# A two-layer hybrid diffusion trunk: branch A's GpSimd instructions placed on VectorE and ScalarE

## The chip, the cores and the metric

The kernel runs on one core of a Trainium2 chip. Its time is the device time of one execution in microseconds (us). Five engines work side by side, each through its own queue in order: TensorE (PE, with its weight loads shown as PEld), VectorE (DVE), ScalarE (ACT), GpSimd (POOL) and SyncE (SP, which issues most DMAs). An engine waits on semaphores for what another engine or a DMA must deliver. Before the change the median of three runs is 2233.82 us (2230.44 to 2238.89).

## The reference

One inference step of two trunk layers over 384 tokens (128 of context, 256 latent) with 2048 features in fp32. Each layer modulates its input, multiplies it by one wide input projection, feeds three branches, gates them, joins them, multiplies by an output projection and normalises. Cut to what matters here:

```python
u = x * (1.0 + scale[:, None]) + shift[:, None]
proj = jnp.matmul(u, lp['w_in'])            # 2048 x 8976
y_a = rwkv_mixer(...)    # A: 8 heads x 64, two directions
y_b = mlstm_mixer(...)   # B: 4 heads x 128, two directions
y_c = diff_attn_mixer(...)  # C: 8 heads, two softmaxes each
out = jnp.matmul(jnp.concatenate([y_a, y_b, y_c], axis=-1), lp['w_out'])
x_new = layer_norm(DEEPNORM_ALPHA * x + gate[:, None] * out, ...)

# branch A, one direction, one token (rwkv_scan):
sk = jnp.einsum('bhvk,bhk->bhv', S, kk_t)
S = S * w_t[:, :, None, :] - sk[..., None] * (kk_t * a_t)[:, :, None, :] + v_t[..., None] * k_t[:, :, None, :]
y_t = jnp.einsum('bhvk,bhk->bhv', S, r_t)
# and, beside the scan, the product of the same position:
bonus = bonus + jnp.sum(r * kt * lp['rwkv_r_k'], axis=-1, keepdims=True) * v
```

## The kernel before, in words

The two projections carry nearly all of the arithmetic. Their fp32 weights arrive in pieces of 512 KB (tile `raw`). ScalarE rounds half a piece to fp32r (`hi<-raw`) and VectorE, or for every fourth half piece GpSimd, takes the remainder (`lo<-raw,hi`). TensorE then makes three products for each block, hi times hi, hi times lo and lo times hi, into an accumulator `acc`; they are called the large products here. Everything else that TensorE does writes to a rotating PSUM tile `mx`, apart from the modulation (`ada`).

Branch A turns the token by token scan into chunks of 64 tokens. A unit is one chunk in one direction; there are 6 chunks and 2 directions, so 12 units in each layer and 24 in all. A unit passes through four streams, each of which may run ahead of the next:

- `a_front` (stream AF, line 1048) makes the decays (`th`, `q`), their products with the keys and values (tiles named `GE` and `QH` in the rows) and the product of the same position (`Tt`, `ci`, `big`), multiplies them on TensorE and masks the result into `Xo` and `Xd`. After its twelfth unit it scales four blocks and multiplies them with `VC`, which gives the bonus.
- `a_blocks` (AD, line 1166) inverts 8x8 blocks on VectorE by a chain of small instructions (`own`, `Xc`, `xr`, `tm`, `Di`).
- `a_inverse` (AI, line 1195) extends that to 64x64 by small matmuls, ScalarE copies and VectorE sums (tile `mixed`).
- `a_scan` (A, line 1236) carries the state `S` and adds up the output.

Before the change GpSimd makes the products for the upper 64 partitions of `GE` and `QH`, the product of the same position, the two differences `Xo - Xd` and `Xd - own`, and the copies into `LP` (the inputs of a unit) and `UV` (its values).

The order in which the instructions stand in the queues is found while the program is built. Every instruction passes through line 155, so all rows carry that line and are told apart by tile names. A planner (`spend`, line 265) keeps one clock for each engine with a price for each kind of instruction (`cost`, line 237). After each piece of the large products, `pump` (line 372) places a segment of a waiting stream (C's attention, A's four streams, evacuations) if its engine is free by these clocks, and places none while VectorE's or ScalarE's clock is more than `SLACK` ahead of TensorE's (line 377). At a few places the order is forced: `drain` (line 407) runs the ready streams, oldest first and with no large product between them, until the named stream has ended. One such place is `b_first` (line 1443), which calls `drain("AF")` because branch B's queries take the memory of `KR` that `a_front` reads. It stands in each layer behind the last key projection of C. The prices for VectorE, ScalarE and GpSimd differ, so moving an instruction to another engine changes the order of everything that the planner places.

Of the kernel before, what the change touches and what calls it, by code (L numbers as in the profile page):

```python
# [15 lines left out]
OP = mybir.AluOpType  # L16
# [34 lines left out]
PESHARE = 2000.0, 2000.0  # L51
HEAD = ("PG", 2), ("QHt", 2), ("Tt", 2), ("BK", 1), ("QH", 1), ("UV", 1), ("ce00", 1), ("ce10", 1)
MIX = "cccqqqvvvvq", "cccqqqvvvvq"
# [73 lines left out]
def bc(ap, shape):  # L127
    return ap.to_broadcast(list(shape))
# [73 lines left out]
class Hybrid:  # L202
# [845 lines left out]
    def a_front(self):  # L1048

        nc = self.nc  # L1050
        rev = slice(None, None, -1)
        lo, hi = slice(0, 64), slice(64, 128)
        fl = lambda x: x.rearrange("p a b -> p (a b)")

        def inputs(u):
            d, c = self.A_ORDER[u]
            for j, r in enumerate((lo, hi)):
                nc.gpsimd.tensor_copy(self.LP[r, j, :], self.LW[r, d, 64 * c:64 * c + 64])

        inputs(0)  # L1060

        wait = [self.mt([128, 4, 64], "Tt", bufs=2) for _ in range(2)]
        wait += [self.KR[:, :, 0, 64 * i:64 * i + 64] for i in range(2)]
        first = {}
        yield
        for u, (d, c) in enumerate(self.A_ORDER):
            ts = slice(64 * c, 64 * c + 64)
# [19 lines left out]
            BK = self.mt([128, 4, 2, 64], "BK")  # L1087
# [10 lines left out]
            Ea = E[:, :, d:64 + d], E[:, :, 1 - d:65 - d]  # L1098
            EQ = self.mt([128, 4, 64], "q1")
# [3 lines left out]

            PG = self.mt([128, 4, 4, 64], "GE", bufs=2)
            pgv = PG[lo, 0:3:2], PG[hi, 1:3]
            for e, r in enumerate((lo, hi)):
                (nc.gpsimd if e else nc.vector).tensor_tensor(PG[r, e], Ea[0][r], self.KR[r, :, 0, ts], OP.mult)
            nc.vector.tensor_tensor(PG[:, 2], Ea[1], self.KR[:, :, 1, ts], OP.mult)
            WL = self.mt([128, 4], "WL", bufs=2)
            self.act(WL, civ[:, :, last], AF.Exp, scale=-DECAY)  # L1110
            QH = self.mt([128, 4, 2, 64], "QH")
            for e, r in enumerate((lo, hi)):
                eqb = bc(EQ[r].unsqueeze(2), [64, 4, 2, 64])
                if e == 0:
                    nc.vector.tensor_tensor(QH[r], eqb, BK[r], OP.mult)
                else:
                    nc.gpsimd.tensor_tensor(QH[r][:, :, rev, :], eqb, BK[r], OP.mult)
            if c not in first:
                pd = first[c] = wait[{0: 0, 1: 1, 2: 0, 5: 1, 3: 2, 4: 3}[c]]
                nc.gpsimd.tensor_tensor(pd, BK[:, :, 1, :], self.KR[:, :, 1, ts], OP.mult)  # L1120
            else:
                pd = self.mt([128, 4, 64], "ci")
                nc.gpsimd.tensor_tensor(pd, BK[:, :, 1, :], self.KR[:, :, 1, ts], OP.mult)
                nc.gpsimd.tensor_tensor(self.KR[:, :, 1, ts], pd, first[c], OP.add)
            if u < 11:
                inputs(u + 1)
            yield
            pg = [self.mxp() for _ in range(2)]
            for p in range(4):
                for e, r in enumerate((lo, hi)):  # L1130
                    nc.tensor.matmul(pg[e][:, 128 * p:128 * p + 128], QH[r, p].rearrange("k a b -> k (a b)"),
                                     pgv[e][:, :, p, :], start=True, stop=True)
            GE = self.mt([128, 2, 4, 64], "PG", bufs=2)
            Xd = self.mt([128, 4, 64], "Xd", bufs=2)
            Xo = self.mt([128, 4, 64], "Xo", bufs=2)
# [8 lines left out]
            pq = [self.mxp() for _ in range(2)]  # L1144
            for e, r in enumerate((lo, hi)):
                for p in range(4):
                    nc.tensor.transpose(pq[e][:, 64 * p:64 * p + 64], QH[r, p].rearrange("k a b -> k (a b)"), self.ident[r, r])
            for e in range(2):
                nc.scalar.copy(QHt[:, e], pq[e][:, 0:256].rearrange("p (a b) -> p a b", a=4))
            bm = bc(self.k("bm16").unsqueeze(1), [128, 4, 64])  # L1150
            nc.vector.tensor_tensor(Xd, Xo, bm, OP.mult)
            nc.gpsimd.tensor_tensor(Xo, Xo, Xd, OP.subtract)
            self.fronts[u] = (Xd, Xo)
            self.units[u] = (PG, GE, QHt, WL)
            self.nf = u + 1
# [10 lines left out]
    def a_blocks(self):  # L1166


        nc = self.nc
        b8 = self.k("bm8")  # L1170
        for u, (d, c) in enumerate(self.A_ORDER):
            Xd, Xo = self.fronts.pop(u)
            own = self.mt([128, 4, 64], "own")
            nc.vector.tensor_tensor(own, Xd, bc(b8.unsqueeze(1), [128, 4, 64]), OP.mult)
            Xc = self.mt([128, 4, 8], "Xc")
            nc.vector.tensor_reduce(Xc, own.rearrange("p a (q t) -> p a t q", q=8), AX.X, OP.add)
            Di = self.mt([128, 4, 8], "Di", bufs=2)
            nc.vector.tensor_copy(Di, bc(self.k("i8").unsqueeze(1), [128, 4, 8]))
            nc.gpsimd.tensor_tensor(Xd, Xd, own, OP.subtract)
            yield  # L1180
            for n, s in enumerate(range(7) if d == 0 else range(7, 0, -1)):
                xr = self.mt([128, 4, 8], "xr")
                nc.vector.stream_shuffle(xr, Xc, [8 * i + s for i in range(4) for _ in range(8)])
                t2 = slice(s + 1, 8) if d == 0 else slice(0, s)
                w = 7 - s if d == 0 else s
                tm = self.mt([128, 4, 8], "tm")
                nc.vector.tensor_tensor(tm[:, :, 0:w], bc(Di[:, :, s:s + 1], [128, 4, w]), xr[:, :, t2], OP.mult)
                nc.vector.tensor_tensor(Di[:, :, t2], Di[:, :, t2], tm[:, :, 0:w], OP.add)
                if n % 3 == 2 and n < 6:
                    yield  # L1190
            self.blocks[u] = (Xd, Xo, Di)
            self.nd = u + 1
            yield
# [42 lines left out]
    def a_scan(self):  # L1236

        nc = self.nc
        lo, hi = slice(0, 64), slice(64, 128)
        ysum = self.mixed[:, 4:8, :]  # L1240
        v4 = lambda x: x.rearrange("p (a b) -> p a b", a=4)
        for u, (d, c) in enumerate(self.A_ORDER):
            ts = slice(64 * c, 64 * c + 64)
            UV = self.mt([128, 2, 4, 64], "UV")
            S = self.S[d, 0 if c < 2 else 1]
            for e, (ur, vr) in enumerate(((lo, hi), (hi, lo))):
                nc.scalar.copy(UV[ur, e], S[ur])
                nc.gpsimd.tensor_copy(UV[vr, e], self.VT[vr, c])
            yield
            PG, GE, QHt, WL, Tt = self.units.pop(u)  # L1250
            pr = self.mxp()
# [253 lines left out]
    def b_main(self):  # L1505
# [17 lines left out]
        nc.vector.tensor_scalar(nf, f, -1.0, None, OP.mult)  # L1523
        gr = [self.mt([4, T], ("QHt", "QH")[d], bufs=(2, 1)[d]) for d in range(2)]
        br = [self.mt([4, T], ("UV", "th")[d]) for d in range(2)]
# [567 lines left out]
```

## Time and profile before

| | |
|---|---|
| median of three runs | 2233.82 us |
| profiled execution, time | 2234.41 us |
| its span, first to last instruction | 2232.7 us |
| PE / PEld busy | 2131.0 us (95%) / 1875.6 us (84%) |
| DVE / ACT / POOL busy | 1376.1 us (62%) / 950.1 us (43%) / 651.1 us (29%) |
| mean granted TensorE clock | 0.983 of full speed |

Busy times are sums of instruction durations, so a busy PE is not PE at its peak. Branch A's units lie in two stretches, from about 190 to 760 us (layer 0) and from about 1290 to 1810 us (layer 1). In a grouped row the two numbers behind the bar are the sum in us and the mean in ns, and then the engine's idle time just before and what ended it.

### The profile page before, as it was taken

The page shows a single profiled execution, that of the slowest core. Times are in us where ns is not written, and L with a number is a line of the kernel's source. Part 1 is how long each engine was busy: PE and PEld are TensorE (multiplying, and loading weights), DVE is VectorE, ACT ScalarE, POOL GpSimd, SP SyncE. Part 2 cuts the span into 40 slices and gives each one's busy share as a digit, 9 for nine tenths or more (in the row PEclk, how much of TensorE's full clock was granted, in tenths as well). Part 3 has the DMA queues.
Part 4 walks back from the last instruction along what each step waited for, and adds up shares of the span by engine and source line. Part 5 has one row for each costly group of instructions (what it writes and reads, how often), then busy time and mean ns, then how long its engine had stood idle before and what let it go on. Part 6 is the DMA issues. An engine that isn't in the chain of part 4 may idle for free. (4 is left out here: it accounts for less than half of the span.)

```text
span 2232.7 us, 44851 instructions
## 1 busy us (share of the span) xinstructions
PE 2131.0 (95%) x17261; PEld 1875.6 (84%) x17261; DVE 1376.1 (62%) x3704; ACT 950.1 (43%) x2215; POOL 651.1 (29%) x930
## 2 busy tenths in 40 slices
PE   6999999999999999999998999999999999999998
PEld 3778878778778788889997998787888789999997
DVE  2667766766675523578338677776776754367634
ACT  3345344353343533445326453444444354344543
POOL 3111433324332211111435223242343312111344
PEclk9999999999999999999998999999999999999998
DMA  9995433433434464554465442223232224333444
GB/s 323 317 320 148 135 112 110 128 100 108 148 99 137 151 194 155 171 154 152 153 198 185 137 123 91 78 76 105 70 93 79 78 83 152 114 114 118 141 146 144
DMA packets 313791, 314.83 MB, mean 141 GB/s; under 512 B 17569, under 2 KB 309030, under 8 KB 313450
## 3 DMA queue, kind: packets, MB, share of 16 engines
q1 hardware_dynamic: 305450, 299.49, 43.1%
q0 software_dynamic: 3616, 10.22, 1.4%
q8 instruction: 136, 2.23, 0.4%
q10 hardware_dynamic: 4512, 2.26, 0.4%
q14 instruction: 77, 0.63, 0.1%
HBM read 298.81 MB, written 13.12 MB: 140 GB/s over the span
## 5 line engine op out<-in xcount | busy, mean ns | idle before, releaser
L155 PE MATMUL acc<-uh,hi 128*128 128x384 f32 x2240 | 808.0, 361 | 11.6 <-ACT uh L155 7.7
L155 PE MATMUL acc<-uh,lo 128*128 128x384 f32 x2240 | 763.0, 341 | 5.8 <-POOL lo L155 3.4
L155 PE MATMUL acc<-ul,hi 128*128 128x384 f32 x2240 | 762.9, 341 | 1.3 <-DVE ul L155 1.3
L155 DVE TENSOR_TENSOR lo<-raw,hi 128x512 fp32r<-128x512 f32 (+1 forms) x496 | 361.8, 739 | 519.2 <-ACT hi L155 508.7
L155 ACT CAST hi<-raw 128x512 fp32r<-128x512 f32 (+1 forms) x659 | 395.7, 618 | 401.3 <-PE acc L155 259.4
L155 POOL TENSOR_TENSOR lo<-raw,hi 128x512 fp32r<-128x512 f32 (+1 forms) x163 | 221.9, 1361 | 927.3 <-ACT hi L155 860.0
L155 PEld LDWEIGHTS acc<-uh,hi 128*128 128x128 f32 x2240 | 426.6, 190 | 76.4 <-issue 35.8
L155 PEld LDWEIGHTS acc<-uh,lo 128*128 128x128 f32 x2240 | 425.3, 190 | 9.2 <-DVE lo L155 4.9
L155 PEld LDWEIGHTS acc<-ul,hi 128*128 128x128 f32 x2240 | 426.2, 190 | 6.0 <-DVE ul L155 3.1
L155 PE MATMUL acc<-hi,uh 128*128 128x256 f32 (+1 forms) x768 | 226.5, 295 | 2.8 <-ACT hi L155 1.1
L155 PE MATMUL acc<-lo,uh 128*128 128x256 f32 (+1 forms) x768 | 216.8, 282 | 1.0 <-DVE lo L155 1.0
L155 PE MATMUL acc<-hi,ul 128*128 128x256 f32 (+1 forms) x768 | 216.1, 281 | 0.0
L155 PEld LDWEIGHTS acc<-hi,uh 128*128 128x128 f32 x768 | 144.5, 188 | 20.3 <-issue 10.9
L155 PEld LDWEIGHTS acc<-lo,uh 128*128 128x128 f32 x768 | 144.6, 188 | 1.8 <-DVE lo L155 1.8
L155 PEld LDWEIGHTS acc<-hi,ul 128*128 128x128 f32 x768 | 144.7, 188 | 0.0
L155 ACT ACTIVATE ce<-mx,cmx 128x384 f32<-128x384 f32 (+1 forms) x96 | 48.0, 505 | 113.2 <-DVE cmx L155 110.1
L155 PE MATMUL ada<-raw,sil 128*32 128x256 f32 x1088 | 88.4, 399 | 1.8 <-DMA raw<-in_w_ada_dram 1.8
L155 ACT COPY mixed<-mx 64x256 f32<-64x256 f32 x120 | 44.0, 366 | 104.4 <-PE mx L155 102.7
L155 PEld LDWEIGHTS mx<-mixed 128*64 128x64 f32 x1536 | 53.5, 139 | 26.3 <-issue 11.1
L155 PE MATMUL mx<-mixed 128*64 128x64 f32 x1536 | 66.9, 230 | 3.3 <-DVE mixed L155 2.9
L155 DVE TENSOR_TENSOR mixed<-mx,mixed 128x256 f32<-128x256 f32 (+1 forms) x96 | 40.1, 418 | 30.1 <-PE mx L155 29.7
L155 DVE TENSOR_REDUCE cmx<-mx 128x1 f32<-128x384 f32 (+1 forms) x96 | 40.4, 460 | 19.8 <-PE mx L155 19.5
(435 smaller groups left out, 2940.5 us busy)
## 6 DMA issues: line engine op xcount, KB each, us to landing
raw<-in_w_in_dram SPq DMA_DIRECT2D x224, 512.0 KB
raw<-in_w_ada_dram SPq DMA_DIRECT2D x136, 512.0 KB
raw<-in_w_out_dram SPq DMA_DIRECT2D x64, 512.0 KB
big<-in_w_ada_dram SPq DMA_DIRECT2D x42, 512.0 KB
raw<-in_w_in_dram SPq DMA_DIRECT2D x32, 520.0 KB
GE<-in_w_ada_dram SPq DMA_DIRECT2D x14, 512.0 KB
cq<-xs SPq DMA_DIRECT2D x32, 192.0 KB
big<-in_w_in_dram SPq DMA_DIRECT2D x21, 256.0 KB
```

Of the source, the lines that this page charges most:

```text
L155: r = f(*args, **kw)
```

## The change

Branch A has no instruction on GpSimd any more apart from clearing. VectorE now makes `GE` and `QH` for all 128 partitions at once, the product of the same position and both differences. ScalarE copies the upper half of `GE` and of `QH` into the order that the matmul of the upper half reads (`QH` has three parts for it), and makes the copies into `LP` and `UV`. The shapes that TensorE reads stay as they are.

```diff
--- before.py
+++ after.py
@@ -1055,7 +1055,7 @@
         def inputs(u):
             d, c = self.A_ORDER[u]
             for j, r in enumerate((lo, hi)):
-                nc.gpsimd.tensor_copy(self.LP[r, j, :], self.LW[r, d, 64 * c:64 * c + 64])
+                nc.scalar.copy(self.LP[r, j, :], self.LW[r, d, 64 * c:64 * c + 64])
 
         inputs(0)
 
@@ -1103,32 +1103,30 @@
 
             PG = self.mt([128, 4, 4, 64], "GE", bufs=2)
             pgv = PG[lo, 0:3:2], PG[hi, 1:3]
-            for e, r in enumerate((lo, hi)):
-                (nc.gpsimd if e else nc.vector).tensor_tensor(PG[r, e], Ea[0][r], self.KR[r, :, 0, ts], OP.mult)
+            nc.vector.tensor_tensor(PG[:, 0], Ea[0], self.KR[:, :, 0, ts], OP.mult)
+            nc.scalar.copy(PG[hi, 1], PG[hi, 0])
             nc.vector.tensor_tensor(PG[:, 2], Ea[1], self.KR[:, :, 1, ts], OP.mult)
             WL = self.mt([128, 4], "WL", bufs=2)
             self.act(WL, civ[:, :, last], AF.Exp, scale=-DECAY)
-            QH = self.mt([128, 4, 2, 64], "QH")
-            for e, r in enumerate((lo, hi)):
-                eqb = bc(EQ[r].unsqueeze(2), [64, 4, 2, 64])
-                if e == 0:
-                    nc.vector.tensor_tensor(QH[r], eqb, BK[r], OP.mult)
-                else:
-                    nc.gpsimd.tensor_tensor(QH[r][:, :, rev, :], eqb, BK[r], OP.mult)
+
+            QH = self.mt([128, 4, 3, 64], "QH")
+            nc.vector.tensor_tensor(QH[:, :, 0:2, :], bc(EQ.unsqueeze(2), [128, 4, 2, 64]), BK, OP.mult)
+            nc.scalar.copy(QH[hi, :, 2, :], QH[hi, :, 0, :])
+            qh = lambda e, p: QH[(lo, hi)[e], p, e:e + 2, :].rearrange("k a b -> k (a b)")
             if c not in first:
                 pd = first[c] = wait[{0: 0, 1: 1, 2: 0, 5: 1, 3: 2, 4: 3}[c]]
-                nc.gpsimd.tensor_tensor(pd, BK[:, :, 1, :], self.KR[:, :, 1, ts], OP.mult)
+                nc.vector.tensor_tensor(pd, BK[:, :, 1, :], self.KR[:, :, 1, ts], OP.mult)
             else:
                 pd = self.mt([128, 4, 64], "ci")
-                nc.gpsimd.tensor_tensor(pd, BK[:, :, 1, :], self.KR[:, :, 1, ts], OP.mult)
-                nc.gpsimd.tensor_tensor(self.KR[:, :, 1, ts], pd, first[c], OP.add)
+                nc.vector.tensor_tensor(pd, BK[:, :, 1, :], self.KR[:, :, 1, ts], OP.mult)
+                nc.vector.tensor_tensor(self.KR[:, :, 1, ts], pd, first[c], OP.add)
             if u < 11:
                 inputs(u + 1)
             yield
             pg = [self.mxp() for _ in range(2)]
             for p in range(4):
                 for e, r in enumerate((lo, hi)):
-                    nc.tensor.matmul(pg[e][:, 128 * p:128 * p + 128], QH[r, p].rearrange("k a b -> k (a b)"),
+                    nc.tensor.matmul(pg[e][:, 128 * p:128 * p + 128], qh(e, p),
                                      pgv[e][:, :, p, :], start=True, stop=True)
             GE = self.mt([128, 2, 4, 64], "PG", bufs=2)
             Xd = self.mt([128, 4, 64], "Xd", bufs=2)
@@ -1144,12 +1142,12 @@
             pq = [self.mxp() for _ in range(2)]
             for e, r in enumerate((lo, hi)):
                 for p in range(4):
-                    nc.tensor.transpose(pq[e][:, 64 * p:64 * p + 64], QH[r, p].rearrange("k a b -> k (a b)"), self.ident[r, r])
+                    nc.tensor.transpose(pq[e][:, 64 * p:64 * p + 64], qh(e, p), self.ident[r, r])
             for e in range(2):
                 nc.scalar.copy(QHt[:, e], pq[e][:, 0:256].rearrange("p (a b) -> p a b", a=4))
             bm = bc(self.k("bm16").unsqueeze(1), [128, 4, 64])
             nc.vector.tensor_tensor(Xd, Xo, bm, OP.mult)
-            nc.gpsimd.tensor_tensor(Xo, Xo, Xd, OP.subtract)
+            nc.vector.tensor_tensor(Xo, Xo, Xd, OP.subtract)
             self.fronts[u] = (Xd, Xo)
             self.units[u] = (PG, GE, QHt, WL)
             self.nf = u + 1
@@ -1176,7 +1174,7 @@
             nc.vector.tensor_reduce(Xc, own.rearrange("p a (q t) -> p a t q", q=8), AX.X, OP.add)
             Di = self.mt([128, 4, 8], "Di", bufs=2)
             nc.vector.tensor_copy(Di, bc(self.k("i8").unsqueeze(1), [128, 4, 8]))
-            nc.gpsimd.tensor_tensor(Xd, Xd, own, OP.subtract)
+            nc.vector.tensor_tensor(Xd, Xd, own, OP.subtract)
             yield
             for n, s in enumerate(range(7) if d == 0 else range(7, 0, -1)):
                 xr = self.mt([128, 4, 8], "xr")
@@ -1245,7 +1243,7 @@
             S = self.S[d, 0 if c < 2 else 1]
             for e, (ur, vr) in enumerate(((lo, hi), (hi, lo))):
                 nc.scalar.copy(UV[ur, e], S[ur])
-                nc.gpsimd.tensor_copy(UV[vr, e], self.VT[vr, c])
+                nc.scalar.copy(UV[vr, e], self.VT[vr, c])
             yield
             PG, GE, QHt, WL, Tt = self.units.pop(u)
             pr = self.mxp()
```

VectorE's queue at the first unit of layer 0, difference of the two programs (`q` holds the inverse decays, `big` the normalised keys and the receptance, `BK` the scaled keys):

```order
 L155 SCALAR_TENSOR_TENSOR BK_2390<-BK_2390,big_343_1767 128x4x64
 L155 SCALAR_TENSOR_TENSOR BK_2390<-th_2308,big_342_1766 128x4x64
-L155 TENSOR_TENSOR GE_2426<-th_2394,big_342_1766 64x256
-L155 TENSOR_TENSOR GE_2426<-th_2394,big_342_1766 128x256
-L155 TENSOR_TENSOR QH_2432<-q_448_2397,BK_2390 64x512
+L155 TENSOR_TENSOR GE_2426<-th_2394,big_342_1766 128x256 x2
+L155 TENSOR_TENSOR QH_2432<-q_448_2397,BK_2390 128x4x128
+L155 TENSOR_TENSOR Tt_2301<-BK_2390,big_342_1766 128x256
 L155 TENSOR_TENSOR lo_2448<-raw_2377,hi_2447 128x512
 L155 TENSOR_TENSOR lo_2452<-raw_2377,hi_2451 128x512
```

Two 64-partition products became parts of 128-partition ones, and the product of the same position (`Tt`) stands on VectorE ahead of the next remainders (`lo`).

ScalarE's queue at the same unit, after the change:

```order
L155 ACTIVATE q_448_2397<-ci_2352 128x256
L155 COPY GE_2426<-GE_2426 64x256
L155 ACTIVATE WL_2430<-ci_2352 128x4
L155 COPY QH_2432<-QH_2432 64x4x64
L155 COPY LP_1770<-mixed_1765 64x64 x2
L155 CAST hi_2447<-raw_2377 128x512
```

The four copies (one each into `GE` and `QH`, two into `LP`) are new on this queue and stand ahead of the next rounding (`hi`).

TensorE's queue at the forced place in layer 1, behind the last key projection of C, before the change (`mx` are small matmuls, here a step of A's inverse; `ada` the modulation; `acc` the large products):

```order
L155 MATMUL acc_20655<-ul_126,hi_20878 128x384
L155 MATMUL acc_20655<-uh_125,lo_20879 128x384
L155 MATMUL mx_21014<-mixed_14454 64x64 x8
L155 MATMUL ada_19307<-raw_20652,sil 32x256 x4
L155 MATMUL acc_21053<-uh_125,hi_20908 128x384
L155 MATMUL acc_21053<-ul_126,hi_20908 128x384
L155 MATMUL acc_21053<-uh_125,lo_20909 128x384
```

Eight small matmuls and four of the modulation stand between two large products.

The same place after the change, twelve rows from the middle of what stands between the same two large products (`ce`, `ck`, `cq` and `cvv` belong to C's attention, `mixed`, `UV`, `GE` and `big` to A):

```order
L155 MATMUL mx_20889<-mixed_14454 64x64 x8
L155 MATMUL mx_20899<-const,ce_4073_20842 128x128
L155 MATMUL mx_20906<-mixed_14454 64x64 x8
L155 MATMUL mx_20916<-big_2793_14455,const 128x384
L155 MATMUL mx_20919<-cvv_19914,ce_4074_20844 128x128
L155 MATMUL mx_20923<-const,ce_4086_20880 128x128
L155 MATMUL mx_20926<-mixed_14454 64x64 x8
L155 MATMUL mx_20951<-ck_20742,cq_20366 128x384
L155 MATMUL mx_20952<-ck_20742,cq_20366 128x384
L155 MATMUL mx_20962<-cvv_19914,ce_4087_20882 128x128
L155 MATMUL mx_20966<-UV_20936,GE_20260 64x64 x8
L155 MATMUL mx_20976<-big_2793_14455,const 128x384
```

`a_front` has not ended there, so the drain runs: 130 small matmuls and four of the modulation now stand between the two large products. It is the longest such run in either program; the longest in A's part of the program before has 36.

## Rows read from the trace of the kernel before

**Rows 1.** The page, part 1: busy us, share of the span, instructions.
```profile
PE 2131.0 (95%) x17261; PEld 1875.6 (84%) x17261; DVE 1376.1 (62%) x3704; ACT 950.1 (43%) x2215; POOL 651.1 (29%) x930
```

**Rows 2.** Windows of A's stretches: us, busy PE PEld DVE ACT POOL, PEclk, DMA, GB/s.
```profile
190.00:760.00 570.00, 545.42 (x5332) 454.44 (x5330) 384.15 (x1112) 241.79 (x634) 176.61 (x286) 0.99 0.41 123
...
1290.00:1810.00 520.00, 492.73 (x4808) 429.52 (x4807) 372.65 (x1053) 224.62 (x594) 177.04 (x284) 0.99 0.29 88
...
250.00:300.00 50.00, 46.55 (x463) 39.98 (x464) 36.61 (x108) 16.53 (x42) 18.27 (x25) 0.93 0.37 115
1650.00:1700.00 50.00, 47.70 (x404) 41.38 (x403) 34.73 (x100) 23.61 (x71) 15.08 (x18) 0.97 0.31 94
```

**Rows 3.** Waits of PE, layer 0's stretch: us in total, times, longest us.
```profile
PE mx L155 <- DVE mixed L155: 6.8, 5, 2.7
PE mx L155 <- DVE GE L155: 3.6, 6, 1.5
PE acc L155 <- ACT hi L155: 3.3, 4, 1.4
```

**Rows 4.** Waits of PE, layer 1's stretch.
```profile
PE mx L155 <- DVE mixed L155: 7.3, 7, 3.2
PE mx L155 <- DVE GE L155: 3.6, 5, 1.4
```

**Rows 5.** Tiles QH and GE: count, min/median/max ns, first and last start.
```profile
L155 DVE TENSOR_TENSOR QH<-q,BK x24: 673/696/1220, 229.4 to 1743.1; 64x512 f32<-64x512 f32 x24
...
L155 DVE TENSOR_TENSOR GE<-th,big x48: 375/904/1518, 228.8 to 1742.2; 64x256 f32<-64x256 f32 x24, 128x256 f32<-128x256 f32 x24
L155 DVE TENSOR_TENSOR GE<-mx,const x48: 406/417/428, 235.7 to 1748.0; 64x256 f32<-64x256 f32 x48
```

**Rows 6.** Timeline of DVE at 1498 to 1507: start us, us, instruction.
```profile
1500.42 2.34 DVE L155 TENSOR_TENSOR GE<-th,big 64x256 f32<-64x256 f32 x2
1502.69 1.17 DVE L155 TENSOR_TENSOR QH<-q,BK 64x512 f32<-64x512 f32 x1
...
1504.01 1.03 DVE L155 TENSOR_TENSOR tm<-Di,xr 128x16 f32<-128x16 f32 x1
...
1506.23 0.17 DVE L155 TENSOR_TENSOR tm<-Di,xr 128x8 f32<-128x8 f32 x1
```

**Rows 7.** Timeline of POOL in the same stretch.
```profile
1502.57 0.75 POOL L155 TENSOR_TENSOR GE<-th,big 64x256 f32<-64x256 f32 x1
1503.28 1.73 POOL L155 TENSOR_TENSOR QH<-q,BK 64x512 f32<-64x512 f32 x1
```

**Rows 8.** Timeline of PE behind it, and at 237 to 240 us.
```profile
1508.84 0.68 PE L155 MATMUL mx<-mixed,Xd 64*64 64x64 f32 x16 [3.22 <-DVE mixed L155]
...
237.55 0.47 PE L155 MATMUL mx<-const,QH 64*128 64x64 f32 x8
...
239.09 1.05 PE L155 MATMUL mx<-LP,lora 128*128 128x128 f32 x8
```

**Rows 9.** Window of the 3.4 us that follow the stall.
```profile
1509.90:1513.30 3.40, 3.40 (x37) 2.85 (x33) 1.06 (x3) 0.98 (x2) 1.26 (x1) 0.50 0.80 248
```

**Rows 10.** DVE groups by shape, 1290 to 1810: busy us, mean ns, idle before.
```profile
L155 DVE STREAM_SHUFFLE xr<-Xc 128x32 f32<-128x32 f32 x84 | 15.7, 186 | 0.0
L155 DVE TENSOR_REDUCE cmx<-mx 128x1 f32<-128x384 f32 x28 | 14.3, 550 | 3.5 <-PE mx L155 3.5
...
L155 DVE SCALAR_TENSOR_TENSOR ce<-ce,cf,ce 128x384 f32<-128x384 f32 x13 | 9.2, 709 | 0.5
...
L155 DVE TENSOR_TENSOR GE<-mx,mixed 128x256 f32<-128x256 f32 x12 | 5.0, 418 | 2.3 <-PE mx L155 2.2
...
L155 DVE TENSOR_TENSOR VC<-mx,VC 128x384 f32<-128x384 f32 x4 | 2.2, 554 | 1.3 <-PE mx L155 1.3
```

**Rows 11.** ACT groups by shape, the whole span.
```profile
L155 ACT COPY UV<-S 64x256 f32<-64x256 f32 x48 | 19.3, 402 | 12.1 <-DMA out_dram<-UV 11.6
```

**Rows 12.** The page, part 5: POOL's costliest group.
```profile
L155 POOL TENSOR_TENSOR lo<-raw,hi 128x512 fp32r<-128x512 f32 (+1 forms) x163 | 221.9, 1361 | 927.3 <-ACT hi L155 860.0
```

## The prediction on record

> **What bounds the kernel now.** I read the page's busy times first, then the windows of the two stretches in which branch A's units lie, then TensorE's waits in them, then the timeline before the longest of these waits. TensorE is busy for 2131 of 2232.7 us and no other engine is above 62% [rows 1], so the end moves only by what TensorE loses: gaps, and time at its lower clock. In A's stretches it is busy 545.4 of 570 us and 492.7 of 520 [rows 2], so it idles 24.6 + 27.3 = 51.9 us there, half of its idle time in the whole span. VectorE is busy 384 and 373 us in them, 67% and 72%; it is late at places, but not full. Of the gaps, 6.8 + 3.6 us in layer 0 and 7.3 + 3.6 us in layer 1 are waits for VectorE's `mixed` (A's inverse) and `GE` (A's products) [rows 3, 4]: 21.3 us. The other 30.6 us are many short waits for other tiles and pieces that no wait explains.
>
> Gaps cost the clock as well. Before the longest stall (3.22 us, PE waiting for `mixed`) [rows 8] TensorE ran at full speed; in the 3.4 us that begin just after it the granted clock is 0.50 [rows 9], which is 1.2 instead of 2.4 GHz. Of the 50 us windows in A's stretches one shows 0.93 and six show 0.97 (the first and the last of the seven stand in rows 2). That is 2 x 50 x (0.07 + 6 x 0.03) = 25 us at half speed, worth at most 12.5 us.
>
> **Why VectorE is late there.** The timeline before that stall shows it. While GpSimd makes its halves of `GE` and `QH` [rows 7], VectorE's two `GE` products take 2.34 us together and its `QH` 1.17 us, and a `tm` instruction of 16 elements a lane takes 1.03 us where one of 8 behind it takes 0.17 [rows 6]. Over the span `GE<-th,big` has a minimum of 375 ns and a median of 904, while `GE<-mx,const`, as long but with one operand in PSUM, stays between 406 and 428 [rows 5]. So a VectorE instruction with both operands in SBUF stretches when GpSimd works, and here GpSimd's own share of A is what stretches it.
>
> The Trainium skill ("SBUF — State Buffer", section "Who interferes with whom") says that a VectorE instruction with two SBUF inputs contends with a GpSimd instruction that reads SBUF, and that the second to start waits for the first to finish. The two `GE` forms of rows 5 agree. The rule speaks for the change as far as A's GpSimd work goes, and against it in that each new VectorE product meets what GpSimd keeps; that is the second case below.
>
> **The change, part by part.**
>
> *Products of decays.* In each of 24 units VectorE made two `GE` products (median 0.90 us each) and `QH` (0.70), 2.50 us. It now makes the same number on 128 partitions. Nothing in the rows makes more partitions dearer, so I price them by the undisturbed minimum, 2 x 0.38 + 0.67 = 1.42 us [rows 5], if GpSimd is quiet, and 2.50 if not. Gain on VectorE 0 to 1.1 us a unit; I take 0.8, nearer to quiet, because their GpSimd partners are gone.
>
> *Moved to VectorE.* 84 instructions of 128x256: `Xd - own`, `Xo - Xd` and the same-position product in every unit, the sum of two such products in every second. At 0.42 us (the nearest row, `GE<-mx,mixed`, 418 ns) [rows 10] that is 84 / 24 x 0.42 = 1.47 us a unit; at the disturbed 0.90 it would be 3.2. VectorE's net is 1.47 - 0.8 = 0.7 us a unit, 8 us a stretch: 69% and 73% busy. It doesn't become the bound.
>
> *Moved to ScalarE.* Six copies a unit, four of 64x256 at 0.40 us (`UV<-S`) [rows 11] and two small ones, not above that: at most 6 x 0.40 x 24 = 58 us on an engine busy 43% [rows 1]. TensorE doesn't read them at once, except the upper halves of `GE` and `QH`, which now come through VectorE and then a copy. PE's largest labelled wait for ScalarE in layer 0's stretch is 3.3 us [rows 3]; I add 2 us, between 0 (copies hidden behind large products) and 19 (both copies bare in all 24 units: 24 x 0.8).
>
> *What TensorE gets back.* At most the 21.3 us of waits for `mixed` and `GE`, and 12.5 us of clock; at least nothing. Half of the waits end in steps in which GpSimd's part of A isn't what is late, since GpSimd keeps its remainders (163 of 1.36 us) [rows 12]. I take half of the waits and a third of the clock: 10.7 + 4.2 = -15 us. Bounds 0 and -34.
>
> *What the new order adds.* TensorE's queue at the forced drain in layer 1 is the term that decides the sign. The order shows 130 small matmuls between two large products where eight stood, because `a_front` has not ended when `b_first` asks for its memory. Behind that drain the whole GEMM is queued, so for its length TensorE has nothing else. Its own work in it: 96 products of 64x64 at 0.47 / 8 us, 30 others of 128 columns or the modulation's at 1.05 / 8, and eight of 384 columns at three times that [rows 8]: 5.6 + 3.9 + 3.2 = 12.7 us, which is needed anyway. VectorE's work in the same section is 72 instructions: 15 of 128x256 (0.42), 8 row maxima (at most 0.55), 4 with `VC` (0.55), 4 sums of exponentials (0.71 at most), 7 steps of the 8x8 inversion (0.19 + 2 x 0.17), the rest about twenty small ones that I price as `xr`, 0.19 [rows 6, 10]: 6.3 + 4.4 + 2.2 + 2.8 + 3.7 + 3.8 = 23 us. So the section can't be shorter than 23 us, and TensorE idles at least 23 - 12.7 = 10 us in it. Nor is VectorE full there: A's inverse and scan go PE, ACT, PE, DVE and back, each step waiting for the one before. At the 73% of the stretch it is 23 / 0.73 = 31 us, a loss of 19. I take 28 us, a loss of 15, and 2 us for the lower clock behind it, as in rows 9: +17 us. Bounds +10 and +24 (half speed throughout the section, with its 12.7 us of matmuls partly hidden).
>
> In layer 0 and elsewhere drains find nearly nothing left. The order of the rest is shifted by up to a few dozen large products; the rows can't price that, I take 0 with 6 us to either side.
>
> Sum against the profiled execution: 2234.4 - 15 + 2 + 17 = 2238 us. The median of the runs is 0.6 us below that execution, so the same number serves for it.
>
> **The other ways.** *The drain outweighs the relief (slower).* Place: the section in layer 1. Price: its 31 us variant, 19 us, and 2 of clock. It decides if less than about 10 us come back elsewhere. For it: the remainders on GpSimd remain, and every one of the 84 new instructions has both operands in SBUF and can meet one. With 5 us back: 2234.4 - 5 + 2 + 21 = 2252. By the rule of the Trainium skill above this is what the remaining readers on GpSimd would do. Against it: the stretches in rows 6 come from A's own GpSimd work.
>
> *The relief outweighs the drain (faster).* If all waits for `mixed` and `GE` go and 8 us of clock with them, and the section takes its shortest 23 us: 2234.4 - 21.3 - 8 + 10 + 2 = 2217. For it: rows 6 to 8, where the 3.22 us stall follows 3.2 us of stretching. Against it: the drain's chain can't be packed to 100% of VectorE.
>
> *ScalarE's copies become the wait.* If in most units TensorE waits for the copies of `GE` and `QH`, 24 x 0.8 = 19 us stand instead of 2: 2238 + 17 = 2255. Against it: in the unit shown the rounding of the next piece stands behind the copies, not ahead.
>
> **How the numbers follow.** My forecast, relief and drain about equal, gets 0.45, its own range 2228 to 2248. The drain outweighing gets 0.30, the relief 0.17, the copies 0.08. A measurement can tell 0.5%, 11 us, from no change. Faster: most of the relief's case and a little of the forecast, 0.17. Slower: most of the drain's and the copies' cases and the forecast's upper edge, 0.37. The rest, 0.46, is within. The range reaches from the relief's to near the copies' time, 2218 to 2255.
>
> **What would show it.** In the new profile, at about 1775 to 1810 us, a hole of 25 to 32 us without `acc` matmuls, TensorE half idle, and a granted clock below 1 in it or right behind; if the hole is under 20 us the drain's price is wrong. `GE<-th,big` and `QH<-q,BK` on VectorE should have medians near 0.42 and 0.70 us; if they stay at 0.9, the remainders are what stretches them and the relief falls. PE's waits for `mixed` and `GE` should halve outside the hole, and TensorE's idle time in layer 0's stretch fall from 24.6 us to 15 to 20. Waits of PE for ScalarE's `GE` or `QH` above 5 us would show the copies. A time above 2255 or below 2218 would mean that the reordering in the rest has a price that I could not see.

## The result and the profile after

The changed kernel takes 2205.84 us (median of 4 runs, 2203.73 to 2208.86) against 2235.04 for before on the same chip: a ratio of 0.9877, 95% interval 0.9852 to 0.9902. The forecast was 2238, its range ended at 2218, and faster had a chance of 0.17. The forecast was wrong. The profiled execution took 2208.86 us with a span of 2207.2.

The page, part 1, of the kernel after (columns as in [rows 1]):

```profile
PE 2124.9 (96%) x17261; PEld 1870.6 (85%) x17261; DVE 1373.9 (62%) x3788; ACT 999.4 (45%) x2359; POOL 491.8 (22%) x702
```

VectorE has 84 instructions more and is busy for 2.2 us less. GpSimd gave up 159 us, ScalarE took 49. The windows of A's two stretches, and of the drain in layer 1 (columns as in [rows 2]):

```profile
190.00:760.00 570.00, 559.76 (x5455) 468.19 (x5454) 399.36 (x1182) 276.01 (x729) 108.40 (x200) 0.99 0.43 130
1290.00:1810.00 520.00, 498.92 (x4788) 433.53 (x4787) 364.92 (x1097) 246.45 (x677) 103.46 (x200) 0.97 0.29 87
...
1728.90:1766.10 37.20, 27.70 (x257) 19.15 (x255) 22.89 (x83) 16.46 (x54) 4.19 (x5) 0.72 0.16 50
```

In layer 0 TensorE's idle time fell from 24.6 us [rows 2] to 10.2. In layer 1 it fell from 27.3 to 21.1, and 9.5 of these lie in the third row, the drain. VectorE's tiles show that the stretching is mostly gone: `GE<-th,big` has a median of 418 ns where the median was 904 [rows 5].

```profile
L155 DVE TENSOR_TENSOR QH<-q,BK x24: 676/684/1780, 229.1 to 1720.8; 128x512 f32<-128x512 f32 x24
...
L155 DVE TENSOR_TENSOR GE<-th,big x48: 383/418/1527, 228.4 to 1720.4; 128x256 f32<-128x256 f32 x48
L155 DVE TENSOR_TENSOR GE<-mx,const x48: 405/416/431, 234.0 to 1726.3; 64x256 f32<-64x256 f32 x48
```

Where the time went is read by position. The 9024 large products stand in the same order in both programs, so the start of the n-th one can be compared. Layer 0's stretch (708th to 2334th) took 504.3 us before and 482.7 after. Of the 21.6 us, 14.0 are idle time of TensorE (23.9 to 9.9) and 5.2 clock (17.1 to 6.8 us at half speed, each worth half). From the 5172nd to the 6816th, layer 1 before its drain, 32.2 us came back: 13.6 are idle time (25.2 to 11.6), 1.7 clock (10.2 to 6.8 us at half speed), and the rest, some 17, are mostly small matmuls that now lie in the drain. Then the drain: the 6817th starts 37.2 us behind the 6816th, where it was 1.5. TensorE is busy for 27.7 of the 37.2 us, 17.7 of these at half clock. So, as an estimate, the section holds 18.8 us of work at full clock, 8.9 us that the half clock adds and 9.5 us of idle time: the drain loses 18.4 us. The rest of the program gained another 7 us, part of it work that the drain had done in advance.

Waits of TensorE over the whole span, after (columns as in [rows 3]):

```profile
PE mx L155 <- ACT ce L155: 10.1, 7, 4.0
PE mx L155 <- DVE GE L155: 3.8, 8, 1.1
PE mx L155 <- DVE mixed L155: 3.3, 9, 0.8
PE acc L155 <- DVE mixed L155: 3.2, 1, 3.2
PE mx L155 <- ACT UV L155: 2.0, 2, 1.8
PE mx L155 <- ACT mixed L155: 0.4, 1, 0.4
```

The small matmuls' waits for `mixed` were 14.1 us in the two stretches [rows 3, 4] and are 3.3; the longest was 3.2 and is 0.8. One wait of 3.2 us for `mixed` now stands before a large product instead. The first row was 4.1 us before, and 8.4 of its 10.1 are the drain's. TensorE in the drain, between the two large products, with its three longest waits:

```profile
1728.94 0.34 PE L155 MATMUL acc<-uh,lo 128*128 128x384 f32 x1
...
1736.07 1.12 PE L155 MATMUL mx<-mixed,Xo 64*64 64x64 f32 x16 [1.79 <-ACT ce L155]
...
1749.17 1.60 PE L155 MATMUL mx<-UV,GE 128*64 128x64 f32 x16 [2.35 <-ACT ce L155]
...
1757.54 1.11 PE L155 MATMUL mx<-mixed,GE 64*64 64x64 f32 x14 [3.96 <-ACT ce L155]
...
1766.14 0.44 PE L155 MATMUL acc<-uh,hi 128*128 128x384 f32 x1
```

By the profile all three end with `ce`, the exponentials of C's attention. The waiting matmuls are A's and don't read `ce`. Each writes into `mx`, which has three buffers, and `ce` reads one of these, so the wait is probably for a buffer to come free (argued, not tested). Before these `ce`, ScalarE had itself been idle for 2.66, 1.74 and 5.61 us, until VectorE had made `cmx`, C's row maxima. The longest of them:

```profile
1755.50 1.01 DVE L155 TENSOR_REDUCE cmx<-mx 128x1 f32<-128x384 f32 x2
1756.55 0.17 DVE L155 TENSOR_SCALAR cmx<-cmx 128x2 f32<-128x2 f32 x1
...
1756.82 0.58 ACT L155 ACTIVATE ce<-mx,cmx 128x384 f32<-128x384 f32 x1 [5.61 <-DVE xr L155]
```

In VectorE's queue three steps of A's inversion stand ahead of these maxima. So VectorE is not full, with 22.9 us of work in the 37.2 (the prediction priced 23), and yet it holds the section up: TensorE waits for ScalarE, and ScalarE for VectorE. 20.5 us of the section run at half clock (mean 0.72).

### The profile page after: what moved, and what is told of

Its sections match the earlier page's. It is cut to its first block, busy times and chain, and to the rows that moved or that the text cites. A ratio compares the mean times of both kernels' runs of the same rounds, so it can differ in the third digit from the quotient of the medians.

```text
span 2207.2 us, 44694 instructions
## 1 busy us (share of the span) xinstructions
PE 2124.9 (96%) x17261; PEld 1870.6 (85%) x17261; DVE 1373.9 (62%) x3788; ACT 999.4 (45%) x2359; POOL 491.8 (22%) x702
## 4 chain that ended last, share of the span: by engine, by line
PE 72%; DVE 14%; DMA 6%; ACT 4%; issue 2%; POOL 1%; SPq 0%; DVEq 0%; ACTq 0%; POOLq 0%
PE acc L155 53%; PE mx L155 16%; DMA raw<-in_w_in_dram 5%; PE ada L155 3%; DVE lo L155 3%; ACT hi L155 2%; DVE mixed L155 1%; DVE cmx L155 1%; DVE big L155 1%; DVE tm L155 1%; ACT ce L155 1%; DVE GE L155 1%; DVE Di L155 1%; DVE xr L155 1%; POOL lo L155 1%
## 5 line engine op out<-in xcount | busy, mean ns | idle before, releaser
L155 PE MATMUL acc<-uh,hi 128*128 128x384 f32 x2240 | 804.0, 359 | 11.1 <-ACT uh L155 7.6
L155 PE MATMUL acc<-ul,hi 128*128 128x384 f32 x2240 | 759.9, 339 | 2.3 <-DVE ul L155 2.3
L155 PE MATMUL acc<-uh,lo 128*128 128x384 f32 x2240 | 759.6, 339 | 1.1 <-DVE lo L155 0.5
L155 DVE TENSOR_TENSOR lo<-raw,hi 128x512 fp32r<-128x512 f32 (+1 forms) x496 | 352.1, 720 | 501.9 <-ACT hi L155 496.9
L155 ACT CAST hi<-raw 128x512 fp32r<-128x512 f32 (+1 forms) x659 | 395.3, 618 | 385.1 <-PE acc L155 253.2
L155 PEld LDWEIGHTS acc<-uh,hi 128*128 128x128 f32 x2240 | 424.0, 189 | 69.9 <-issue 29.9
L155 POOL TENSOR_TENSOR lo<-raw,hi 128x512 fp32r<-128x512 f32 (+1 forms) x163 | 220.4, 1352 | 1130.8 <-ACT hi L155 1053.0
L155 PEld LDWEIGHTS acc<-ul,hi 128*128 128x128 f32 x2240 | 423.9, 189 | 6.5 <-DVE ul L155 3.9
L155 PEld LDWEIGHTS acc<-uh,lo 128*128 128x128 f32 x2240 | 422.9, 189 | 3.7 <-DVE lo L155 3.6
L155 PE MATMUL acc<-hi,uh 128*128 128x256 f32 (+1 forms) x768 | 226.8, 295 | 6.3 <-DVE mixed L155 3.2
L155 PE MATMUL acc<-lo,uh 128*128 128x256 f32 (+1 forms) x768 | 217.3, 283 | 1.2 <-DVE lo L155 1.2
L155 PE MATMUL acc<-hi,ul 128*128 128x256 f32 (+1 forms) x768 | 216.5, 282 | 0.0
L155 PEld LDWEIGHTS acc<-hi,uh 128*128 128x128 f32 x768 | 145.0, 189 | 25.2 <-issue 11.7
L155 PEld LDWEIGHTS acc<-lo,uh 128*128 128x128 f32 x768 | 145.0, 189 | 2.2 <-DVE lo L155 2.0
L155 PEld LDWEIGHTS acc<-hi,ul 128*128 128x128 f32 x768 | 145.1, 189 | 0.0
L155 ACT ACTIVATE ce<-mx,cmx 128x384 f32<-128x384 f32 (+1 forms) x96 | 48.0, 505 | 101.8 <-DVE cmx L155 93.3
L155 PE MATMUL ada<-raw,sil 128*32 128x256 f32 x1088 | 87.6, 396 | 2.2 <-DMA raw<-in_w_ada_dram 2.2
L155 PEld LDWEIGHTS mx<-mixed 128*64 128x64 f32 x1536 | 54.1, 140 | 22.4 <-issue 8.7
L155 PE MATMUL mx<-mixed 128*64 128x64 f32 x1536 | 67.7, 231 | 0.7 <-DVE GE L155 0.3
L155 ACT COPY mixed<-mx 64x256 f32<-64x256 f32 x120 | 43.9, 366 | 53.9 <-PE mx L155 52.1
L155 POOL TENSOR_TENSOR gt<-gt,const 128x256 f32<-128x256 f32 x32 | 24.9, 778 | 150.4 <-DVE gt L155 150.3
L155 DVE TENSOR_TENSOR mixed<-mx,mixed 128x256 f32<-128x256 f32 (+1 forms) x96 | 40.1, 417 | 23.9 <-PE mx L155 23.5
```

Source lines behind the costliest of these rows:

```text
L155: r = f(*args, **kw)
```

## The experiments

Two theories at first. **Relief**: what the engines save comes back in any order. **Order**: the planner prices the moved instructions otherwise, its new order of TensorE's queue brings the gain, and the engines are beside the point. The program can be split that way: a helper lets one list of instructions run while the planner prices the other.

```diff
+    def both(self, part, old, new):
+        for eng, op, *args in new if part in MOVE else old:
+            e = getattr(self.nc, eng)
+            getattr(e._e, op)(*args)
+        for eng, op, *args in new if PLAN[self.l] == "new" else old:
...
+            self.spend(getattr(self.nc, eng)._n, op, aps[0], aps[1:], [])
```

Rows of such kernels carry L158 and L1055 or L1056 instead of L155. Each run stands beside runs of the kernel before on its own chip (medians 2236.5 to 2241.0 us), and its ratio is taken against those; between experiments the ratios are compared, not the times. Stretches are those of the one profiled execution of each run: layer 0's as above, layer 1's from the 5172nd to the 6960th large product (515.6 us before, 513.7 after, with its drain).

### The engines without the order, and the order without the engines

`e1_old_order`, everything moved, priced as before. TensorE's and SyncE's queues are those of before.

```diff
+MOVE = 'PR'
+PLAN = ('old', 'old')
```

> The instructions run on the engines of the changed kernel, but the planner prices them as before, so TensorE's order is that of the kernel before and there is no long drain in layer 1. Relief (A's GpSimd instructions held VectorE up): the 22 us won in layer 0's stretch and some 19 us in layer 1's come back without the drain, 2190 to 2200 us. Order (the new order is what won): nothing is won, 2230 to 2240 us.

Measured 2234.1 us, ratio 0.9984 (0.9970 to 0.9997). Relief alone falls: all the engines' work moved, and next to nothing came back (3.6 us by the ratio). Its waits of TensorE:

```profile
PE mx L158 <- ACT mixed L158: 11.8, 10, 2.2
PE mx L158 <- DVE mixed L158: 11.7, 9, 3.0
```

The same stall as in [rows 8], and VectorE ahead of it (columns as in [rows 6]; the last row is GpSimd):

```profile
1504.80 0.68 PE L158 MATMUL mx<-mixed,Xd 64*64 64x64 f32 x16 [2.95 <-DVE mixed L158]
```

```profile
1497.74 0.89 DVE L1055 TENSOR_TENSOR GE<-th,big 128x256 f32<-128x256 f32 x1
1498.54 1.51 DVE L158 TENSOR_TENSOR GE<-th,big 128x256 f32<-128x256 f32 x1
1499.97 0.68 DVE L1055 TENSOR_TENSOR QH<-q,BK 128x512 f32<-128x512 f32 x1
1500.58 0.41 DVE L1055 TENSOR_TENSOR Tt<-BK,big 128x256 f32<-128x256 f32 x1
```

```profile
1498.30 1.47 POOL L158 TENSOR_TENSOR lo<-raw,hi 128x512 fp32r<-128x512 f32 x1
```

Before, `GE` and `QH` took 2.34 + 1.17 = 3.51 us here [rows 6]. Now they take 3.08, since one remainder on GpSimd is enough to hold up the second `GE`, and the added `Tt` takes 0.41: 3.49 together. The small steps behind them are no longer stretched, so from the start of `GE` to the end of `mixed` VectorE needs 6.92 us instead of 8.27. Yet `GE` starts 1.2 us later than before, counted from the small matmuls `mx<-GE,S` that stand ahead of the stall. Among what stands ahead of it on VectorE are an `own` stretched by another remainder and the moved difference:

```profile
1485.00 1.52 DVE L158 TENSOR_TENSOR own<-Xd,const 128x256 f32<-128x256 f32 x1
...
1487.21 0.41 DVE L1055 TENSOR_TENSOR Xd<-Xd,own 128x256 f32<-128x256 f32 x1
```

The stall is 2.95 us instead of 3.22. So what the quiet saves, added and stretched work ahead of it uses up. The second loss is on ScalarE: its copies now stand ahead of its copies of A's inverse, and TensorE waits 11.8 us for these, where before had:

```profile
PE mx L155 <- ACT mixed L155: 1.3, 3, 0.5
```

`e2_old_engines`: before's engines, priced as after. TensorE's and SyncE's queues are those of after, with the drain.

```diff
+MOVE = ''
+PLAN = ('new', 'new')
```

> The instructions run on the engines of the kernel before, the planner prices them as in the changed kernel, so TensorE's order is the changed one, drain included. Relief: slower than before by the drain, 2250 to 2270 us. Order: near the changed kernel, 2205 to 2215 us.

Measured 2234.6 us, 0.9989 (0.9977 to 1.0001): between the two expectations. Order alone falls as well, over the whole. Layer 0's stretch takes 491.8 us, so 12.5 us of its gain are the order's and 9.1 need the engines. Outside the drain the order alone saves some 15 us of idle time and clock (with the changed engines 40), about what its drain loses (13). The wait for `mixed`, 14.2 us over the whole span before and 11.7 in e1, is nearly gone here, with GpSimd's share of A in place. But TensorE now waits for the copies of values that GpSimd makes, which before's trace doesn't show:

```profile
PE mx L158 <- ACT ce L158: 12.8, 11, 4.1
PE mx L158 <- POOL UV L1055: 9.6, 7, 3.0
...
PE mx L158 <- DVE mixed L158: 3.4, 5, 1.6
```

From here a third theory, **Together**: each order places a consumer where the planner thinks its operand is ready, so the engines gain only in an order planned with their prices.

### The same engines in other orders

The planner's price for VectorE is line 260. Four orders more:

```diff
 e5_before_dearer (before)
-            return (0.26 if op == "memset" else 1.042) * n + 69 + 61 * ptr
+            return 1.03 * ((0.26 if op == "memset" else 1.042) * n + 69 + 61 * ptr)
 e7_after_72 (after)
+            return (0.26 if op == "memset" else 1.042) * n + 72 + 61 * ptr
 e8_after_cheaper (after)
+            return 0.97 * ((0.26 if op == "memset" else 1.042) * n + 69 + 61 * ptr)
 e6_before_lat (before)
-LAT = 130.0
+LAT = 135.0
```

> The kernel before, its engines untouched; in the planner every VectorE instruction costs 3% more, so A's segments are placed a little later (the order shows a drain of 9 segments at layer 1's forced place). Price (before, VectorE ran later than the planner believed, because GpSimd stretches it, and the changed kernel brings its time and its price closer): layer 0's stretch gets 5 to 15 us shorter, in all 2218 to 2230 us. Luck (any other order gives another time): layer 0's stretch moves either way by up to 10 us. Both needed (the new order wins only with the new engines): 2230 to 2240 us.

Measured 2227.5, 0.9947 (0.9926 to 0.9968), the time that Price gave, but not at its place: layer 0's stretch takes 501.2 us (504.3 before), and layer 1's 499.9 where it took 515.6. So with the engines untouched one price moves layer 1 by 16 us.

> The kernel before with one number of the planner changed that prices no engine (the delay behind a result, 130 to 135 ns): another order, no more margin for VectorE, no drain. Price: 2230 to 2242 us. Luck: may lie 10 us or more from before.

Measured 2237.7, 0.9998 (0.9978 to 1.0017). The order came out practically as before's (8 of 9025 places between large products differ), so this is only a repeat.

> The changed kernel, a fixed 72 instead of 69 ns in VectorE's price: another order with the same engines, in which no segment is left for the drain in layer 1. Price: layer 0's stretch stays 15 to 25 us shorter than before, and without the drain the whole takes 2180 to 2190 us. Luck: layer 0's stretch moves by 10 us or more from the changed kernel's.

Measured 2195.6 (2192.09 to 2198.24), 0.9806 (0.9782 to 0.9830), the fastest of all, though above the 2190 that was expected: the drain is gone (the 6817th large product starts 2.0 us behind the 6816th), and layer 0 stays at 480.1 us.

> The changed kernel, every VectorE instruction 3% cheaper in the planner: A's segments are placed earlier, no drain is left. Price: half of layer 0's gain goes (10 us), layer 1 saves the drain's 24 us, 2190 to 2205 us. Luck: as e7, with layer 0's stretch as likely to gain as to lose.

Measured 2212.3, 0.9879 (0.9856 to 0.9902), without a drain. Layer 0 stayed at 482.3 us, against the expectation; layer 1 is 17.0 us longer than in `e7_after_72`, and the time is above the range expected. So orders that differ by a few per cent in one price are already 16 us apart.

Then the other engines in the same orders (`e10_old_order_103` has e5's, `e14_old_eng_72` e7's, `e11_old_eng_097` e8's; TensorE's and SyncE's queues are equal in each pair):

> The changed engines, with the order of the run in which before's VectorE price was 1.03 times as dear. Together (the new engines pay only in an order that was planned with their prices): layer 0's stretch 498 to 503 us as with the old engines in that order (501.2), the time 2220 to 2230. Luck (before's own order happens to be poor in layer 0, and most others would do): layer 0's stretch 480 to 490, the time 2203 to 2213.

> Before's engines in the order of the run in which the changed kernel's VectorE price was 0.97 times as dear (no long drain in it). Together: layer 0's stretch 489 to 495 us, as with before's engines in the changed kernel's order (491.8), the time 2222 to 2232. Order alone (the engines add nothing): layer 0's stretch 481 to 485, the time 2209 to 2216.

> Before's engines in the order of the fastest run so far (the changed kernel with VectorE's fixed price at 72, 2195.6 us, no long drain). Together (the engines gain in orders planned for them): 20 to 45 us slower than that run, 2216 to 2241, layer 0's stretch 490 to 502. Order (that order is good in itself): within 10 us of it, 2196 to 2206.

| order planned for | before's engines | changed engines | gain |
|---|---|---|---|
| before's (before, e1) | 1 | 0.9984 | 0.2% |
| before's (e5, e10) | 0.9947 | 0.9915 (0.9892 to 0.9937) | 0.3% |
| the changed (e2, after) | 0.9989 | 0.9877 | 1.1% |
| the changed (e14, e7) | 0.9935 (0.9909 to 0.9960) | 0.9806 | 1.3% |
| the changed (e11, e8) | 1.0071 (1.0049 to 1.0092) | 0.9879 | 1.9% |

The times were 2218.9, 2254.6 and 2224.6 us. Layer 0's stretch took 498.8 us in e10 and 494.8 in e14, as Together said; in e11 the stretch (501.3) and the time were longer than any theory had them. The moved instructions are the same in all five pairs. They are worth 0.2 to 0.3% in the orders planned for the old engines, hardly clear of noise, and 1.1 to 1.9% in those planned for the new. Nor are the new orders better in themselves: with before's engines the five lie around 1. One wait stands out in each mismatch. With before's engines in new orders it is the one for GpSimd's copies of values, here in e11 and then in e14 (no such row in before, after or e7):

```profile
PE mx L158 <- POOL UV L1055: 14.6, 5, 4.1
```

```profile
PE mx L158 <- POOL UV L1055: 9.6, 3, 4.2
```

With the changed engines in old orders it is the one for ScalarE's `mixed`: 11.8 us in e1, and in e10

```profile
PE mx L158 <- ACT mixed L158: 8.8, 9, 2.0
```

In after it is 0.4. These waits are a third or so of the difference within the three new pairs; the rest is not traced to single waits.

`e4_layer1_old_order` takes the new order in layer 0 alone:

```diff
+PLAN = ('new', 'old')
```

> The changed kernel with the prices of before in layer 1 alone: layer 0 keeps the changed order, layer 1 has no long drain. Relief: the drain costs 37 us less 13 us of matmuls, so 24 us are won on the changed kernel, 2180 to 2190 us. Order: layer 1 loses the drain's 24 us and its own gain of about 19, 2198 to 2204 us.

Measured 2201.9, 0.9841 (0.9817 to 0.9865), the time that Order gave: layer 0's stretch 483.5 us, no drain; at the 6960th large product it is 7 us ahead of after. The way is not Order's, though. Layer 1's order came out neither as before's nor as after's (154 of 1789 places between large products differ from before's), and its 500.5 us are 15 less than before's, where Order had no gain. In e1, with the same engines and the same prices in that layer, it takes 517.0. So an order planned with the old prices can suit the changed engines too: Together holds for the five pairs, but the spread between orders, 16 us here and in e5, is not far below the 25 to 43 us that the engines are worth in the new orders.

### Contention put back

GpSimd reads A's tiles again in 64-column pieces, into a tile that nobody reads (work that the reference doesn't need): `e3_pool_beside` in before's order, `e9_new_order_pool` in after's.

```diff
+    def idle_pool(self, k, *ins):
+        for _ in range(k if DUMMY else 0):
...
+                self.nc.gpsimd._e.tensor_tensor(out, *ins, OP.mult)
```

> As e1, and GpSimd again reads A's tiles at the places where it worked before, in pieces of 64 columns that take about as long in sum, into a tile that nobody reads (added work, the result is unchanged). Relief by contention: VectorE's products stretch again and most of e1's gain goes, 2220 to 2240 us. Chain (GpSimd's own results came late, nothing was held up): within 5 us of e1.

> The changed kernel in its own order, with GpSimd also reading A's tiles again in pieces of 64 columns into a tile that nobody reads (work that the reference doesn't need). Contention (what the new engines bring is that GpSimd no longer reads beside VectorE's products): layer 0's stretch goes from 482.7 us back to 490 to 496, the time to 2222 to 2235. Chain (what they bring is that GpSimd's slower instructions no longer stand in A's chain): layer 0's stretch stays at 482 to 486, the time at 2204 to 2212.

`e3_pool_beside` took 2250.3 us, 1.0059 (1.0041 to 1.0077), 16 above e1 and above both expectations. `e9_new_order_pool` took 2223.3, 0.9935 (0.9913 to 0.9957), 13 above after by the ratios, with layer 0's stretch at 493.5 us: Contention's numbers. In layer 0 it puts back 10.8 of the 21.6 us, about what e2 does with the real instructions (9.1). Its `GE<-th,big` on VectorE:

```profile
L1056 DVE TENSOR_TENSOR GE<-th,big x24: 419/505/1528, 227.1 to 1736.4; 128x256 f32<-128x256 f32 x24
L158 DVE TENSOR_TENSOR GE<-th,big x24: 418/539/549, 227.5 to 1736.8; 128x256 f32<-128x256 f32 x24
```

Both are an upper bound: the added reading is 205 us of GpSimd in e3 and 202 in e9, more than the 163 that moving took off it, and it also delays GpSimd's own work.

### Each part alone

The order is planned for exactly what is moved; `e12_products` moves `GE` and `QH`, `e13_rest` all the others.

```diff
+MOVE = 'P'
...
+        for eng, op, *args in new if part in MOVE else old:
```

> Only the products with decays (GE, QH) and their ScalarE copies are moved; differences, same-position products and the copies of inputs and values stay on GpSimd; the order is planned for exactly that. Contention theory (GE and QH on both engines at once is the costly pair): layer 0's stretch 480 to 487 us, the time 2195 to 2212. Rest theory (A's chain through GpSimd's other instructions counts as much): layer 0's stretch 490 to 500, the time 2213 to 2230.

> The other part alone: differences, same-position products and the copies of inputs and values are moved, while GE and QH stay divided between VectorE and GpSimd; the order is planned for exactly that. If GE and QH on both engines at once are what costs, little is gained: layer 0's stretch 492 to 502 us, the time 2222 to 2235. If the copies of values on GpSimd, which TensorE waits for in new orders, are what costs, this part gains too: layer 0's stretch 482 to 490, the time 2205 to 2218.

`e12_products` took 2210.0 us, 0.9873 (0.9852 to 0.9893); `e13_rest` 2204.8, 0.9843 (0.9814 to 0.9873), with layer 0's stretch at 486.5 and 490.2 us: the first expectation of e12, and just outside the edges of the second of e13. Either part brings as much as the whole with its drain, and none has a long drain. In `e13_rest`, GpSimd still makes half of `GE` and `QH`, and yet VectorE's `GE` is hardly stretched (the median was 904 [rows 5]):

```profile
L1055 DVE TENSOR_TENSOR GE<-th,big x24: 375/415/1498, 230.0 to 1721.6; 64x256 f32<-64x256 f32 x24
```

So the pair of products on two engines doesn't by itself cost the time. The traces show why: of the 48 `GE` products on VectorE, 14 overlap GpSimd's `GE` or `QH` in e13 and 17 did before, but 21 overlap any GpSimd instruction where 39 did. Before, those that overlap none take 411 ns at most, and those that overlap one have medians of 910 (64 partitions) and 948 (128). So what `GE` met before was largely GpSimd's other work.

## Why the prediction was wrong

*The step that failed* is "What TensorE gets back", -15 us with bounds of 0 and -34, together with "the order of the rest", taken as 0 with 6 to either side. Outside the drain 21.6 + 32.2 + 7 = 61 us came back, and about 17 of them are only work moved into the drain. That leaves some 44, beyond the bound: 29 us of TensorE's idle time, 11 of clock, and 4 that neither accounts for. Two errors lie in it. The bound counted the waits for two tiles alone. The other 30.6 us of idle time in the stretches, which the prediction left as short waits that no wait explains, does carry labels (in layer 0 24.2 of 24.6 us have one: ScalarE's `hi` 3.3, VectorE's `mod` 3.2, a DMA into `cr` 2.6), and it fell too: in layer 0 the idle time that was not for `mixed` or `GE` went from 14.2 us to about 7.5. And relief and order were summed as if apart. e1 shows that the engines alone return next to nothing, e2 that the order alone returns what its drain costs, and the five pairs that the two gain together. The prediction's last sign fits: a time below 2218 would mean a price of the reordering that it couldn't see.

*The cause given for the stall was not enough.* Rows 6 to 8 were read as "GpSimd's own share of A stretches VectorE, so VectorE is late". The stretching was real: with that share gone, e1 needs 1.35 us less from `GE` to `mixed`. But the stall is 2.95 us instead of 3.22, because VectorE starts later, while in e2, with GpSimd's share in place and the new order, the waits for `mixed` shrink to 3.4 us. So it was the order that removed them, though not every new order does: in e11 they are 10.6.

*The drain* was right in its mechanism, and its loss came out right by luck. The prediction had a section of 28 us with 12.7 of matmuls, 15 of idle time and 2 for the clock, a loss of 17; it took 37.2, with some 18.8, 9.5 and 8.9, a loss of 18.4. The matmuls were priced from a row of transposes (x8, 0.47 us [rows 8]). A product of 64x64 stands in the trace as two records, and eight of them are the x16 that take 0.68 us [rows 8]. The work on VectorE was priced right (23 us, 22.9 measured). What was missed is the clock, at half for 20.5 us. e7, without the drain, is 16 us below after by its ratio.

*VectorE's net* was given as +8 us a stretch. Over the span it was -2.2 for 84 more instructions. These take 37.6 us; `GE` and `QH` give back 18.2 (the prediction had 24 x 0.8 = 19), its remainders 9.4 and `tm` 5.1. The Trainium skill ("Perfetto Trace Analysis", section "Optimizing Scalar/DVE Operations") says that offloading between GpSimd and VectorE may not help, as they share a read port. These two busy times agree: VectorE's is 1376.1 us with GpSimd's help and 1373.9 without.

*ScalarE's copies* were 2 us, with 19 as a rival. In after, TensorE's waits for ScalarE's `UV` and `mixed` are 2.4 us. In before's order (e1) they are 11.8 (1.3 before): the rival was right there, at another tile than it named.

*The rivals.* "The relief outweighs the drain" came nearest, 2217, but with a relief of 29 us and a section of 23; it was some 44 against one of 37.

## What to carry to other kernels

Where a planner sets a static order, moving work to another engine and the new order are one edit: split them (run one, price the other) before either is given credit. A bound on what the bottleneck engine gets back is its whole idle time in those stretches, with the clock that it costs, not the waits for the tiles of the change alone. And look for forced drains after any change of prices: here a fixed price of 72 instead of 69 took a section of 37 us away.

## What the runs showed of the hardware

A single GpSimd remainder of 1.47 us was enough to stretch an overlapping VectorE product with two SBUF operands from 0.42 to 1.51 us, about the remainder's own length (e1). In before and after, the `GE<-th,big` that overlap no GpSimd instruction take 429 ns at most, and all `GE<-mx,const`, with one operand in PSUM, 405 to 431 ns.
